# Up weight sums moved out of the output projection, down sums by whole blocks, residual loaded into the FFN accumulators, FFN memory laid out by first use

## The chip, the cores and the metric

The kernel runs on one core of a Trainium2 chip. The metric is device time in microseconds (us). The shown time before is the median of three runs. The profile is one further execution of the same program.

TensorE (PE) multiplies matrices into PSUM. VectorE (DVE), ScalarE (ACT) and GpSimd (POOL) do elementwise work. All DMAs here are issued from SyncE's queue (SP), in order: a DMA that waits for something holds up every DMA behind it.

## The reference, cut to what matters

One layer of an encoder for 2048 prompt tokens and 32 sample tokens, width 1024, FFN width 4096, all float32:

```python
z = rmsnorm(x, g_mix) @ w_in            # split into attention and GLA inputs
attn_o = sink_attend(...)               # windowed attention, head group A
gla_o, s_final = gla_chunked(...)       # gated linear attention, head group B
h = x + concat([attn_o, g]) @ w_out     # g: normed, gated gla_o
y = h + square(relu(rmsnorm(h, g_ffn) @ w_up)) @ w_down
```

## The kernel before, in words

Every large product is split in a high and a low float32r part (hi*hi, lo*hi, hi*lo). ACT writes the high part (a copy), POOL or DVE the low one (a subtraction).

**Stages.** Attention runs to about 340 us of the span, GLA to 727, the output projection (`op_phase`) to 900, the FFN (`ffn_phase`) to the end.

**The FFN** runs a Strassen-like scheme on 2x2 blocks: 7 products in place of 8. It takes three token groups in turn ("envs", 356, 356 and 328 columns), and for each of them 16 weight blocks of 256 rows of the FFN width. A block has 7 "up" steps U(b,0) to U(b,6), on the token tiles B11, B21, T2, T1, T3, B22, T4, and 7 "down" steps D(b,0) to D(b,6), on squared outputs uB11, uB22, uT1, uT3, uT2, uB21, uT4. A step has 12 products. U(0,0..6) come first; then D(g-1,i) and U(g,i) alternate. PE keeps this order; the order on the other engines is set by a scheduler that simulates the program. In env 0 all weights are loaded and split anew, with the weights of six steps prepared ahead (`AHEAD`).

**Sums of weights.** The scheme needs sums of weight quarters, S1 to S4. POOL makes them. Down sums (`block_sums`, L707, four operations a unit) are made in attention (5 blocks, in quarters of 128 columns), GLA (8 blocks, in halves) and the output projection (3 blocks, in halves), stored to `sd` in HBM and loaded again in the FFN. Up sums of blocks 1 to 8 (`up_sums`, L1161, four operations of 128x512 a block) are made in the output projection and stored to `su`. Those of blocks 0 and 9 to 15 are made in env 0 of the FFN itself (L1416); S2 and S3 are stored, S1 and S4 are made again in envs 1 and 2 by two operations.

**Output projection.** Six groups of columns, (p, gi) for three pieces and two halves. `post(p, gi)` normalizes a group; the second part of `post(p, 1)` writes the FFN's token tiles T1 to T4, B22 (and B11, B21 after gi = 0) to HBM (`Td`). That of the last group, `post(2,1)`, is left to the first steps of the FFN (`pending`) and uses the PSUM tiles `opa` and `opb`. The residual y goes to `yd`.

**FFN accumulators.** `P1` to `P7` (128x1424 each) take the down products. A first block copies into P2 to P5 (DVE, L1603), later ones add (DVE, L1509). `residual` (L1636, L1639) adds y from `yd` to P2 to P5 in blocks 2 to 9: 8 loads of 356 KB and 10 POOL additions an env. At an env's end `merge` (L1609, POOL) combines the accumulators and 16 stores write `out_yT`.

**Memory.** Pools are stacked: a tile laid on a pool that is gone waits for the last use of what lay there. Before, T1 and T2 lie over the mixer tiles, B11 and B21 over the first ones of these, T3, B22 and T4 over the projection's weights, and the first five slots of the ring of FFN weights (`wring`, pool `wfb`) over `opx`, where the stages of the up sums are. So the ring's first weights wait until the last `su` store has landed.

Of the kernel before, what the change touches and what calls it, by code (L numbers as in the profile page):

```python
# [62 lines left out]
class Builder:  # L63
# [641 lines left out]
    def block_sums(self, raw):  # L705

        tt = lambda o, x, y, op: self.G.tensor_tensor(out=o, in0=x, in1=y, op=op)  # L707
        a11, a21, a12, a22 = raw[:, 0, 0], raw[:, 0, 1], raw[:, 1, 0], raw[:, 1, 1]
        tt(a22, a21, a22, ALU.add)
        tt(a21, a11, a21, ALU.subtract)  # L710
        tt(a11, a22, a11, ALU.subtract)
        tt(a12, a12, a11, ALU.subtract)

    def down_sums(self, units, tile_, gap):

        w = self.a["w_down"].rearrange("(b k p) (m n) -> b p k m n", k=2, p=P, m=2)
        for b, c0, n in units:
            raw = tile_(f"sd{b}_{c0}")[:, : 4 * n].rearrange("p (k m n) -> p k m n", k=2, m=2)
            for k in range(2):
                self.Q.dma_start(raw[:, k], w[b, :, k, :, c0 : c0 + n])  # L720
            yield gap / 2
            self.block_sums(raw)
            yield gap / 2
# [423 lines left out]
    def up_raw(self, b, tile_=None):  # L1147

        w = self.a["w_up"].rearrange("(k p) n -> p k n", p=P)
        H = KB // 2  # L1150
        raw = []
        for k in range(2):
            x = (tile_ or self.io_tile)("stage").rearrange("p (k c) -> p k c", k=H)
            self.last_load = self.Q.dma_start(x, w[:, H * k : H * k + H, 256 * b : 256 * b + 256]).ins
            raw.append(x)
        return raw

    def up_sums(self, raw):

# [647 lines left out]
```

## Time and profile before

| | us |
|---|---|
| runs shown | 2284.13, 2289.86, 2290.94; median 2289.86 |
| profiled execution | 2278.04 |
| its span | 2276.1 |
| PE busy in the span | 2139.4 (94%) |
| DVE, ACT, POOL busy | 1577.8, 1230.9, 1436.6 |
| PE busy, 727 to 900 (output projection) | 168.18 of 173 |
| PE busy, 900 to 972 | 20.28 of 72 |

A row of the timeline gives start, length, engine, line, operation, output<-inputs and how many were merged; in brackets stands how long the engine was idle before it, and what ended that. The granted clock (PEclk) is a share of 2.4 GHz.

### The profile page before, as it was taken

The page shows a single profiled execution, that of the slowest core. Times are in us where ns is not written, and L with a number is a line of the kernel's source. Part 1 is how long each engine was busy: PE and PEld are TensorE (multiplying, and loading weights), DVE is VectorE, ACT ScalarE, POOL GpSimd, SP SyncE. Part 2 cuts the span into 40 slices and gives each one's busy share as a digit, 9 for nine tenths or more (in the row PEclk, how much of TensorE's full clock was granted, in tenths as well). Part 3 has the DMA queues.
Part 4 walks back from the last instruction along what each step waited for, and adds up shares of the span by engine and source line. Part 5 has one row for each costly group of instructions (what it writes and reads, how often), then busy time and mean ns, then how long its engine had stood idle before and what let it go on. Part 6 is the DMA issues. An engine that isn't in the chain of part 4 may idle for free.

```text
span 2276.1 us, 40775 instructions
## 1 busy us (share of the span) xinstructions
PE 2139.4 (94%) x14790; PEld 2007.6 (88%) x14790; DVE 1577.8 (69%) x3444; ACT 1230.9 (54%) x2728; POOL 1436.6 (63%) x1308
## 2 busy tenths in 40 slices
PE   7999999899989997399999998999999999999997
PEld 6777776788878997399999998999999999999996
DVE  8766666799896545457777777576666666676677
ACT  4555445556563222455666655666656666666662
POOL 5221356454462553646678779877787798788884
PEclk9999999899999999699999999999999999999999
DMA  7333576254435998654444448554444476555433
GB/s 267 138 119 107 197 229 196 94 172 140 152 120 176 326 339 317 235 189 153 155 150 136 130 134 302 178 158 152 150 142 131 139 288 194 163 161 155 157 108 117
DMA packets 245771, 402.03 MB, mean 177 GB/s; under 512 B 44721, under 2 KB 173026, under 8 KB 241730
## 3 DMA queue, kind: packets, MB, share of 16 engines
q1 hardware_dynamic: 245570, 399.44, 53.2%
q8 instruction: 116, 1.90, 0.3%
q14 instruction: 85, 0.70, 0.1%
HBM read 300.20 MB, written 99.18 MB: 175 GB/s over the span
## 4 chain that ended last, share of the span: by engine, by line
PE 54%; DVE 2%; DMA 2%; POOL 1%; ACT 0%; issue 0%; SPq 0%; ACTq 0%; POOLq 0%
PE dn L156 27%; PE u L156 27%; DVE P L1509 1%; DVE wf_d15A L1391 0%; DMA B22l<-Td2B 0%; DMA T3l<-Td0T 0%; DMA stage<-in_w_down 0%; DVE P L1609 0%; DMA Td2T<-y 0%; DMA ku0S<-wf_u0S 0%; DMA stage<-sd 0%; DVE u L1509 0%; POOL wf_u0S L1391 0%; DMA su<-stage 0%; POOL stage L1416 0%
## 5 line engine op out<-in xcount | busy, mean ns | idle before, releaser
L1509 DVE TENSOR_TENSOR P<-P,dn 128x712 f32<-128x712 f32 (+1 forms) x642 | 559.7, 875 | 234.7 <-PE dn L156 218.6
L43 ACT ACTIVATE u<-u 128x356 f32<-128x356 f32 (+1 forms) x384 | 174.1, 454 | 38.3 <-PE u L156 22.0
L707 POOL TENSOR_TENSOR sd<-sd 128x256 f32<-128x256 f32 (+1 forms) x168 | 110.7, 668 | 99.7 <-DMA sd<-in_w_down 93.4
L43 ACT ACTIVATE r<-u 128x356 f32<-128x356 f32 (+1 forms) x192 | 88.4, 461 | 136.3 <-PE u L156 136.2
L1509 DVE TENSOR_TENSOR u<-u,r 128x356 f32<-128x356 f32 (+1 forms) x144 | 75.7, 526 | 117.3 <-PE u L156 115.4
L938 POOL TENSOR_TENSOR E<-cc 128x256 f32<-128x256 f32 (+1 forms) x117 | 72.0, 648 | 67.3 <-DVE cc L790 43.5
L1014 DVE COPY_PREDICATED AT<-masks,A 64x64 f32<-64x64 int32 (+1 forms) x330 | 82.9, 253 | 14.2 <-ACT AT L43 4.7
L1609 POOL TENSOR_TENSOR P<-P,P 128x712 f32<-128x712 f32 (+1 forms) x38 | 64.9, 1728 | 26.3 <-DVE P L1509 26.1
L43 ACT ACTIVATE P<-S,negm 128x192 f32<-128x192 f32 (+2 forms) x128 | 51.5, 417 | 46.0 <-DVE negm L577 38.4
L595 POOL TENSOR_TENSOR P<-P,es 128x512 f32<-128x512 f32 x15 | 15.9, 1059 | 87.0 <-ACT sq L43 44.2
L1161 POOL TENSOR_TENSOR stage<-stage 128x512 f32<-128x512 f32 x32 | 42.9, 1344 | 43.0 <-DMA Td1T<-y 21.6
L43 ACT ACTIVATE E<-E 128x1024 f32<-128x1024 f32 (+2 forms) x68 | 67.3, 1012 | 2.8 <-POOL E L938 1.1
L949 DVE TENSOR_TENSOR E<-E,kq 128x256 f32<-128x256 f32 (+1 forms) x117 | 65.5, 615 | 1.1 <-ACT E L43 1.0
L1291 DVE TENSOR_TENSOR y<-op,y 128x356 f32<-128x356 f32 (+1 forms) x48 | 23.7, 517 | 58.0 <-PE op L156 37.8
L1416 POOL TENSOR_TENSOR stage<-stage 128x512 f32<-128x512 f32 x44 | 57.0, 1294 | 10.4 <-DMA stage<-in_w_up 5.0
L43 ACT ACTIVATE v<-go 128x256 f32<-128x256 f32 (+1 forms) x34 | 12.8, 380 | 75.7 <-DVE Sp L1046 43.3
L43 ACT ACTIVATE pS<-pT 128x256 f32<-128x256 f32 (+1 forms) x62 | 27.2, 489 | 46.9 <-PE pT L160 46.9
L576 DVE TENSOR_REDUCE mx<-S 128x2 f32<-128x384 f32 (+2 forms) x64 | 32.7, 536 | 26.8 <-PE S L156 26.5
L1509 DVE TENSOR_TENSOR u<-u,f 128x356 f32<-128x356 f32 (+1 forms) x96 | 49.8, 519 | 0.3 <-ACT u L43 0.2
L43 ACT ACTIVATE op<-y 128x356 f32<-128x356 f32 (+1 forms) x42 | 19.0, 466 | 50.3 <-DVE y L1291 50.3
L156 PE MATMUL u<-B11h,wf_u0A 128*128 128x356 f32 (+1 forms) x24 | 7.8, 392 | 38.3 <-ACT wf_u0A L43 37.9
L43 ACT ACTIVATE f<-u 128x356 f32<-128x356 f32 (+1 forms) x96 | 43.7, 455 | 0.0
(1899 smaller groups left out, 8820.9 us busy)
## 6 DMA issues: line engine op xcount, KB each, us to landing
stage<-in_w_up SPq DMA_DIRECT2D x108, 512.0 KB, 4.4
stage<-sd SPq DMA_DIRECT2D x92, 512.0 KB, 4.8
stage<-su SPq DMA_DIRECT2D x62, 512.0 KB, 4.0
...
```

The source lines that it names most:

```text
L43: ins = f(*args, **kw)
L156: self._pe(self.T.matmul(out, lhsT, rhs, start=start, stop=stop, **kw), ns)
L576: V.reduce_max(mx[:, ch, us], sp, axis=AX.X)
L707: tt = lambda o, x, y, op: self.G.tensor_tensor(out=o, in0=x, in1=y, op=op)
L938: G.tensor_tensor(out=e4, in0=c4, in1=ref, op=ALU.subtract)
L949: V.tensor_tensor(out=e4, in0=e4, in1=halves_of(kq, L, m), op=ALU.mult)
L1014: V.copy_predicated(dst, mk.unsqueeze(1).broadcast_to([L // nh, 2, w // m, m]), src[r].rearrange("s p (n m) -> s p n m", m=m),)
L1161: tt = lambda o, x, y, op: self.G.tensor_tensor(out=o, in0=x, in1=y, op=op)
L1291: V.tensor_tensor(out=y[:, f], in0=ps, in1=y[:, f], op=ALU.add)
L1416: tt = lambda o, x, y, op: G.tensor_tensor(out=o, in0=x, in1=y, op=op)
L1509: add = lambda out, x, y, op=ALU.add: V.tensor_tensor(out=out, in0=x, in1=y, op=op)
L1609: eng.tensor_tensor(out=e.acc[q][:, j : j + 2], in0=e.acc[q][:, j : j + 2], in1=e.acc[x][:, j : j + 2], op=ALU.add)
```

## The change

- Down sums: attention makes 4 blocks instead of 5, begun at step 3 instead of 9, with each POOL operation spawned by itself; GLA 6 instead of 8, in whole blocks (8 operations of 128x256 behind one pair of loads, one buffer); the output projection 6 instead of 3, in whole blocks (4 + 4 operations of 128x512 half a group apart).
- `up_raw` and `up_sums` are gone from the output projection with their 16 loads, 32 POOL operations and 16 stores. Blocks 1 to 8 are now made like 0 and 9 to 15, in the FFN: in env 0 four more POOL operations and one `su` store a block, in envs 1 and 2 two more POOL operations and one load less.
- `post` writes T2 and T4 into the group's own y0 tile, T3 into a buffer shared with z. The store of y[p][1]'s upper half is replaced by z = y_upper - y_lower, 12 new POOL operations of 128x356 in the projection.
- FFN pools are laid out by first use: T1 and T2 over the weights w_out half 0, T3 and B22 over half 1, T4 over the mixer tiles, the ring over `opx` (now two whole-block buffers).
- The residual is loaded into P2 to P5 by four DMAs of 712 KB (656 KB in env 2) an env at block 0, and block 0 of these four adds instead of copying. 8 loads and 10 POOL additions an env go.
- In block 15 of env 0 the low parts of A11 and A12 are made on POOL instead of DVE.

```diff
-EARLY, MIDDLE = 5, 8
+EARLY, MIDDLE = 4, 6
...
-            late = [(b, c0, 256) for b in range(EARLY, EARLY + MIDDLE) for c0 in (0, 256)]
-            two = lambda name: sums.tile([P, 1024], F32, tag="sd", name=name)
-            for j in range(2):
-                self.spawn(self.down_sums(late[j::2], two, 32000), 4000 + 16000 * j)
+            whole = lambda name: sums.tile([P, 2048], F32, tag="sd", name=name)
+            self.spawn(self.down_sums([(b, 0, 512) for b in range(EARLY, EARLY + MIDDLE)], whole, 2, 4500), 4000)
...
-                S.activation(t2[:, k], B, AF.Copy)
-                tt(t4[:, k], y0[:, H + k], B)
-            for x, src in (("T2", t2), ("T1", y[:, :H]), ("T3", t3), ("B22", y[:, H:]), ("T4", t4)):
+                S.activation(y0[:, k], B, AF.Copy)
+                tt(y0[:, H + k], y0[:, H + k], B)
+            for x, src in (("T2", y0[:, :H]), ("T4", y0[:, H:]), ("T1", y[:, :H]), ("T3", t3), ("B22", y[:, H:])):
...
-        todo += [("u", b, 0) for b in range(1, 9)]
...
+        for n, b in enumerate(range(EARLY + MIDDLE, self.NB)):
+            at = KB + 4 * n
+            steps.setdefault(at, []).append(lambda b=b: begin(b))
+            for i in (2, 3):
+                steps.setdefault(at + i, []).append(lambda b=b: more(b))
+            steps.setdefault(at + 6, []).append(lambda b=b: end(b))
...
+                        G.tensor_tensor(out=z[:, f - H], in0=y[:, f - H], in1=y[:, f], op=ALU.subtract)
...
+            tmem = tok(pool("toka"), ("T2", "T1"))
...
+            tmem |= tok(pool("tokb"), ("T3", "B22"))
+            wfa = pool("wfa")
...
+            tmem |= tok(pool("tokd"), ("B11", "B21"))
             wfc = pool("wfc")
-            wfb, sx = pool("wfb"), pool("sx")
+            amem |= {i: mem(pool(f"acc{i}"), H * NM, f"P{i}", F32) for i in (3, 5, 7, 6, 2, 4)}
+            umem["T4"] = upair(pool("ud"), "T4")
+            wfb, xa, sx = pool("wfb"), pool("xa", bufs=2), pool("sx")
...
-                    eng = V if n == 0 and i in (0, 5) else G
+                    eng = V if n == 0 and i in (0, 5) and not keep else G
...
-                        if b:
+                        if b or q not in (1, 6, 7):
                             add(at, at, ps)
...
+                if b or i not in (0, 1, 4, 5):
                     return
...
+                q = DOWN[i + 1][2]
+                gi, f0 = {2: (0, 0), 3: (1, 0), 4: (0, H), 5: (1, H)}[q]
+                Q.dma_start(envs[n].acc[q], self.yd[envs[n].p][gi][:, f0 : f0 + H])
```

Three places show how the order moves, all on SP.

First the end of the output projection. `su` are the stored up sums, `ku0` are stores of split weights of block 0 for the later envs, `stage` are loads of raw weights. SP before:

```order
L59 DMA T3l_10874<-Td1T3_201 128x1424 [waits DMAHW7_49]
L59 DMA B22l_10876<-Td1B22_202 128x1424 [waits DMAHW0_49]
L59 DMA stage_10362<-in_w_up 128x4x256 [waits DMAHW1_49]
L59 DMA T4l_10878<-Td1T4_203 128x1424 [waits DMAHW2_49]
L59 DMA ku0A22_11051<-wf_u0A22_11048 128x1024 [waits DMAHW3_49,Pool_49]
L59 DMA stage_10472<-in_w_up 128x4x256 [waits DMAHW4_49]
L59 DMA stage_10474<-in_w_up 128x4x256 [waits DMAHW5_49]
L59 DMA su70_166<-stage_10360 128x1024 [waits DMAHW6_49,Pool_49]
L59 DMA su71_167<-stage_10362 128x1024 [waits DMAHW7_49,DMAHW1_49,Pool_49]
L59 DMA su80_168<-stage_10472 128x1024 [waits DMAHW4_49,DMAHW0_49,Pool_49]
L59 DMA su81_169<-stage_10474 128x1024 [waits DMAHW5_49,Pool_49]
L59 DMA ku0A11_10950<-wf_u0A11_10947 128x1024 [waits DMAHW2_49,DMAHW6_49,DMAHW1_49,DMAHW7_49,DMAHW0_49,Pool_49]
```
SP after, same place:

```order
L59 DMA T2l_10721<-Td1T2_199 128x1424 [waits DMAHW6_49,PE_49]
L59 DMA T1l_10723<-Td1T1_200 128x1424 [waits DMAHW7_49]
L59 DMA Td2B21_205<-y20_9863 128x1424 [waits DMAHW0_49,DVE_49]
L59 DMA T3l_10741<-Td1T3_201 128x1424 [waits DMAHW1_49,PE_49]
L59 DMA B22l_10743<-Td1B22_202 128x1424 [waits DMAHW2_49]
L59 DMA yd21_189<-y21_10289 128x1424 [waits DMAHW4_49,DMAHW3_49,DVE_49]
L59 DMA T4l_10756<-Td1T4_203 128x1424
L59 DMA yd21_189<-z2_10607 128x1424 [waits DMAHW5_49,Pool_49]
L59 DMA ku0S4_10857<-wf_u0S4_10854 128x1024 [waits DMAHW6_49,Pool_49]
L59 DMA ku0A22_10928<-wf_u0A22_10925 128x1024 [waits DMAHW7_49,Pool_49]
L59 DMA stage_11605<-in_w_up 128x4x256 [waits DMAHW0_49]
L59 DMA su10_154<-stage_11010 128x1024 [waits DMAHW1_49,Pool_49]
```
The eight `su` stores and the loads for them are gone from between T4l and the first weights' stores; T2l and T1l, and then T3l, now wait for PE, yd21 and z2 stand around T4l.

Second the end of `post(2,1)`, some 60 to 70 us later in the span before. Td2 are the stores of its results, P the accumulators. SP before:

```order
L59 DMA Td2B22_209<-y21_10437 128x1424 [waits DMAHW4_49,DVE_49]
L59 DMA Td2T3_208<-tT3_9244 128x1424 [waits DMAHW5_49,DVE_49]
L59 DMA Td2T1_207<-y21_10437 128x1424 [waits DMAHW6_49,Activation_49]
L59 DMA Td2T2_206<-tT2_9243 128x1424 [waits DMAHW7_49,Activation_49]
L59 DMA Td2T4_210<-tT4_9245 128x1424 [waits DMAHW0_49,DVE_49]
L59 DMA stage_11287<-in_w_down 128x1024 [waits DMAHW1_49,DVE_49]
L59 DMA stage_11401<-in_w_down 128x512 [waits DMAHW3_49,DMAHW2_49,Pool_49]
```
SP after:

```order
L59 DMA Td2B22_209<-y21_10289 128x1424 [waits DMAHW3_49,DVE_49]
L59 DMA Td2T3_208<-T32_10698 128x1424 [waits DMAHW4_49,DVE_49]
L59 DMA Td2T1_207<-y21_10289 128x1424 [waits DMAHW5_49,Activation_49]
L59 DMA Td2T2_206<-y20_9863 128x1424 [waits DMAHW6_49,Activation_49]
L59 DMA Td2T4_210<-y20_9863 128x1424 [waits DMAHW7_49,DVE_49]
L59 DMA P4_10805<-yd10_186 128x1424 [waits DMAHW4_49,DMAHW0_49,PE_49]
L59 DMA P2_10801<-yd10_186 128x1424 [waits DMAHW5_49,DMAHW3_49,DMAHW1_49]
L59 DMA stage_11283<-in_w_down 128x512 [waits DMAHW2_49,Pool_49]
L59 DMA P3_10785<-yd11_187 128x1424 [waits DMAHW7_49,DMAHW6_49]
L59 DMA P5_10789<-yd11_187 128x1424
```
The four loads P<-yd now follow the Td2 stores, the last two of them wait for the queue slots of the last stores, and stage loads follow.

Third the change from env 0 to env 1, where the results of env 0 are stored. SP before:

```order
L59 DMA out_yT_prompt<-P3_10931 128x356 [waits DMAHW5_49,Pool_49]
L59 DMA out_yT_prompt<-P3_10931 128x356 [waits DMAHW6_49]
L59 DMA out_yT_prompt<-P2_10930 128x356 [waits DMAHW7_49,DVE_49]
L59 DMA out_yT_prompt<-P2_10930 128x356 [waits DMAHW0_49]
L59 DMA out_yT_prompt<-P3_10931 128x356 [waits DMAHW1_49,Pool_49]
L59 DMA out_yT_prompt<-P3_10931 128x356 [waits DMAHW2_49]
L59 DMA stage_16083<-in_w_down 128x1024 [waits DMAHW3_49,Pool_49]
L59 DMA out_yT_prompt<-P5_10933 128x356 [waits DMAHW4_49,Pool_49]
L59 DMA out_yT_prompt<-P5_10933 128x356 [waits DMAHW5_49]
```
SP after:

```order
L59 DMA out_yT_prompt<-P3_10785 128x356 [waits DMAHW5_49,Pool_49]
L59 DMA out_yT_prompt<-P3_10785 128x356 [waits DMAHW6_49]
L59 DMA out_yT_prompt<-P2_10801 128x356 [waits DMAHW7_49,DVE_49]
L59 DMA out_yT_prompt<-P2_10801 128x356 [waits DMAHW0_49]
L59 DMA out_yT_prompt<-P3_10785 128x356 [waits DMAHW1_49,Pool_49]
L59 DMA out_yT_prompt<-P3_10785 128x356 [waits DMAHW2_49]
L59 DMA P2_10801<-yd20_188 128x1424 [waits DMAHW4_49,DMAHW7_49,DMAHW3_49,DMAHW0_49]
L59 DMA P3_10785<-yd21_189 128x1424 [waits DMAHW5_49,DMAHW6_49,DMAHW2_49,DMAHW1_49]
L59 DMA stage_15872<-sd0_136 128x1024 [waits Pool_49]
L59 DMA out_yT_prompt<-P5_10789 128x356 [waits Pool_49]
```
The loads of P2 and P3 stand between the stores and wait for them; stage loads, and the stores of P5 and P4, are behind.

## Rows read from the trace of the kernel before

**Rows 1.** Stages of the span: busy time of each engine (with instruction counts), granted PE clock, share of the DMA engines' time, GB/s.
```profile
0.00:340.00 340.00, 322.81 (x1804) 252.49 (x1805) 233.08 (x843) 167.41 (x511) 122.25 (x204) 0.98 0.52 176
340.00:727.00 387.00, 354.86 (x3839) 300.13 (x3838) 318.73 (x963) 213.80 (x417) 196.39 (x259) 0.96 0.45 146
727.00:900.00 173.00, 168.18 (x1071) 167.44 (x1069) 88.84 (x222) 42.97 (x84) 79.92 (x66) 0.99 0.94 317
900.00:972.00 72.00, 20.28 (x101) 19.02 (x100) 24.60 (x51) 25.44 (x49) 41.58 (x31) 0.62 0.70 272
1385.00:1445.00 60.00, 49.34 (x286) 48.07 (x286) 40.47 (x49) 33.99 (x68) 55.33 (x39) 0.94 0.75 265
```

**Rows 2.** Timeline of PE from the projection's last product to the step D(0,2).
```profile
899.78 0.32 PE L156 MATMUL op<-mx1h,wo11l 128*128 128x356 f32 x1
...
938.04 0.67 PE L156 MATMUL u<-B11h,wf_u0A 128*128 128x356 f32 x1 [37.94 <-ACT wf_u0A L43]
...
942.53 1.26 PE L156 MATMUL oprb<-ones,acc 128*89 128x1 f32 x8
...
972.42 0.67 PE L156 MATMUL dn<-uB11h,wf_d0A 128*128 128x356 f32 x1 [13.81 <-ACT wf_d0A L43]
...
979.30 0.33 PE L156 MATMUL dn<-uB22h,wf_d0S 128*128 128x356 f32 x1
...
983.19 0.32 PE L156 MATMUL dn<-uT1h,wf_d0S 128*128 128x356 f32 x1
```

**Rows 3.** Timeline of ACT, POOL and SP in the first of these gaps.
```profile
921.55 1.48 ACT L43 ACTIVATE T4h<-T4l 128x712 fp32r<-128x712 f32 x2 [1.59 <-DMA T4l<-Td1T]
937.37 1.15 ACT L43 ACTIVATE wf_u0A<-stage 128x512 fp32r<-128x512 f32 x2 [14.34 <-DMA su<-stage]
927.01 7.59 POOL L1161 TENSOR_TENSOR stage<-stage 128x512 f32<-128x512 f32 x6
928.29 6.66 SPq L59 DMA_DIRECT2D su<-stage  x4
```

**Rows 4.** Timeline of DVE (first and last operation of the second part of `post(2,1)`), SP (its last two stores) and ACT (the first operation behind them).
```profile
950.84 0.59 DVE L1225 SCALAR_TENSOR_TENSOR opa<-y,packed,oprb 128x356 f32<-128x356 f32 x1 [0.37 <-PE oprb L156]
967.89 0.53 DVE L1237 TENSOR_TENSOR tT<-y,opb 128x356 f32<-128x356 f32 x1 [0.53 <-ACT tT L43]
967.89 1.73 SPq L59 DMA_DIRECT2D Td2T<-tT  x2
975.47 0.47 ACT L43 ACTIVATE uT3h<-u 128x356 fp32r<-128x356 f32 x1 [3.10 <-DMA Td2T<-tT]
```

**Rows 5.** DMA issues: KB each and median us from issue to landing, the first row from 896 to 984 us, the others from 1360 to 1450 us.
```profile
T4l<-Td1T SPq DMA_DIRECT2D x1, 712.0 KB, 13.6
...
out_yT_prompt<-P SPq DMA_DIRECT2D x16, 178.0 KB, 3.1
...
B11l<-Td2B SPq DMA_DIRECT2D x1, 712.0 KB, 4.0
...
T4l<-Td2T SPq DMA_DIRECT2D x1, 712.0 KB, 8.6
```

**Rows 6.** Timeline of PE and DVE at the first product of the projection's last group that waited.
```profile
888.12 0.43 PE L156 MATMUL op<-mx1h,wo10h 128*128 128x356 f32 x1 [1.54 <-DVE y L1291]
887.53 2.27 DVE L1291 TENSOR_TENSOR y<-op,y 128x356 f32<-128x356 f32 x5 [6.70 <-DMA y<-in_xT_prompt]
```

**Rows 7.** GLA: who waited for whom (us in total, times, longest), and groups by line (count, busy us, mean ns).
```profile
PE dk L160 <- DVE AT L961: 9.5, 3, 5.8
POOL sd L707 <- DMA sd<-in_w_down: 71.2, 11, 21.1
L707 POOL TENSOR_TENSOR sd<-sd 128x256 f32<-128x256 f32 (+1 forms) x89 | 63.1, 715 | 74.7 <-DMA sd<-in_w_down 71.2
L949 DVE TENSOR_TENSOR E<-E,kq 128x256 f32<-128x256 f32 (+1 forms) x117 | 65.5, 615 | 1.1 <-ACT E L43 1.0
```

**Rows 8.** Timeline of PE, DVE and SP at the change from env 0 to env 1, and of PE at that from env 1 to env 2 (last row).
```profile
1392.62 0.60 PE L156 MATMUL dn<-uB22h,wf_d15S 128*128 128x356 f32 x2 [2.55 <-POOL wf_d15S L1391]
1401.17 9.38 DVE L1391 TENSOR_TENSOR wf_d15A<-stage,wf_d15A 128x512 fp32r<-128x512 f32 x1
1411.41 0.67 PE L156 MATMUL dn<-uT2h,wf_d15S 128*128 128x356 f32 x1 [7.13 <-DVE P L1509]
1402.96 3.38 POOL L1507 TENSOR_TENSOR T4l<-T4l,T4h 128x712 fp32r<-128x712 f32 x2
1426.83 8.40 SPq L59 DMA_DIRECT2D out_yT_prompt<-P  x8
1841.40 0.40 PE L156 MATMUL dn<-uB22h,wf_d15S 128*128 128x356 f32 x1 [1.26 <-ACT B22h L43]
```

**Rows 9.** Durations by line (ns shortest/median/longest, first and last start), and one stretch of env 0 with blocks whose up sums are made there (columns as in rows 1).
```profile
L1416 POOL TENSOR_TENSOR stage<-stage x44: 1273/1294/1313, 841.6 to 2214.4; 128x512 f32<-128x512 f32 x44
L1636 POOL TENSOR_TENSOR P<-P,stage x24: 1591/1725/2126, 1036.5 to 2118.9; 128x712 f32<-128x712 f32 x16, 128x656 f32<-128x656 f32 x8
L1603 DVE COPY P<-dn x24: 841/899/901, 980.5 to 1890.2; 128x712 f32<-128x712 f32 x16, 128x656 f32<-128x656 f32 x8
L1509 DVE TENSOR_TENSOR P<-P,dn x642: 824/895/899, 1003.9 to 2266.5; 128x712 f32<-128x712 f32 x107, 128x656 f32<-128x656 f32 x54
1275.00:1300.00 25.00, 25.00 (x156) 25.00 (x155) 18.42 (x28) 14.66 (x32) 18.42 (x15) 1.00 0.40 133
```

More of the change, by code (lines that the diff above doesn't have):

```diff
@@ L703, in load_gla_consts, with block_sums, load_block, down_sums @@
         self.gla_consts = masks, d0, wal, bal, one, ones
[L705 to L714, printed above, removed]
+    def block_sums(self, raw, parts=1):
+        n = raw.shape[-1] // parts
+        for i in range(parts):
+            part = raw[:, :, :, i * n : (i + 1) * n]
+            a11, a21, a12, a22 = part[:, 0, 0], part[:, 0, 1], part[:, 1, 0], part[:, 1, 1]
+            for o, x, y, op in ((a22, a21, a22, ALU.add), (a21, a11, a21, ALU.subtract), (a11, a22, a11, ALU.subtract), (a12, a12, a11, ALU.subtract)):
+                self.G.tensor_tensor(out=o, in0=x, in1=y, op=op)
+                yield
+    def load_block(self, raw, b, c0, n):
         w = self.a["w_down"].rearrange("(b k p) (m n) -> b p k m n", k=2, p=P, m=2)
+        for k in range(2):
+            self.Q.dma_start(raw[:, k], w[b, :, k, :, c0 : c0 + n])
+    def down_sums(self, units, tile_, parts, step):
         for b, c0, n in units:
             raw = tile_(f"sd{b}_{c0}")[:, : 4 * n].rearrange("p (k m n) -> p k m n", k=2, m=2)
[L719 to L723, printed above, removed]
+            self.load_block(raw, b, c0, n)
+            yield 6000
+            for _ in self.block_sums(raw, parts):
+                yield step
+            yield 6000
             with self.tc.issue_after(self.Q.last.ins):
@@ L1145, in size @@
         return sum(t1 - t0 for _, t0, t1 in g)
[L1147 to L1158, printed above, removed]
-        A = lambda m, k: raw[k - 1][:, :, (m - 1) * P : m * P]
-        tt = lambda o, x, y, op: self.G.tensor_tensor(out=o, in0=x, in1=y, op=op)
-        tt(A(2, 2), A(2, 1), A(2, 2), ALU.add)
-        tt(A(2, 1), A(1, 1), A(2, 1), ALU.subtract)
-        tt(A(1, 1), A(2, 2), A(1, 1), ALU.subtract)
-        tt(A(1, 2), A(1, 2), A(1, 1), ALU.subtract)
     def keep_sums(self, b, raw):
@@ L1176, in op_phase @@
         nt, H = self.nt, KB // 2
[L1177 to L1178 removed]
+        m1 = pool("opm1", 1)
         mem1 = [m1.tile([P, KB * REST + 272], F32R, tag=x, name=f"mx1{x}") for x in "hl"]
@@ L1294, in op_phase @@
                     V.tensor_tensor(out=acc, in0=acc, in1=ps, op=ALU.add)
-                if f % H == H - 1:
-                    hs = slice(f - H + 1, f + 1)
-                    Q.dma_start(self.yd[p][gi][:, hs], y[:, hs])
+                if gi and f >= H:
+                    if f == H:
+                        z = stage(f"z{p}", N)
+                    G.tensor_tensor(out=z[:, f - H], in0=y[:, f - H], in1=y[:, f], op=ALU.subtract)
+                if f == H - 1 and not gi:
+                    Q.dma_start(self.yd[p][gi][:, :H], y[:, :H])
+                if f == KB - 1:
+                    if gi:
+                        Q.dma_start(self.yd[p][gi][:, :H], z)
+                    Q.dma_start(self.yd[p][gi][:, H:], y[:, H:])
                 if f in (1, 2) and pending is not None:
@@ L1303, in op_phase @@
                     next_mix(*groups[j + 1])
-                if j and f in (1, 3, 5, 7):
-                    sums()
-            pending = post(p, gi, acc)
-        while raws:
-            sums()
+                for step in steps.pop(KB * j + f, ()):
+                    step()
+            pending = post(p, gi, acc, stage(f"T3{p}", N) if gi else None)
         self.pending = pending
@@ L1653, in ffn_phase @@
                 else:
+                    residual(g, i)
                     down(g, i)
```

91 lines of the change are left out of this document (28 added, 63 removed).

## The prediction

> **What bounds the kernel now.** First the stages [rows 1]: PE is the bound nearly everywhere and stands still in few places. In attention and GLA it misses 340.00 − 322.81 = 17.2 and 387.00 − 354.86 = 32.1 us; in the projection 4.8. Between 900 and 972 us it works 20.28 us of 72, at a granted clock of 0.62 (near the lower level, 1.2 GHz), and at the change of env 49.34 of 60. So one hole of some 60 us, one of 10, and many small ones are all there is to win.
>
> Then the timeline of PE in the hole [rows 2]. I call the end of the projection E = 900.1 (899.78 + 0.32). U(0,0) starts at 938.04 after 37.94 us, D(0,0) at 972.42 after 13.81 us more, and the regular alternation is reached with D(0,2) at 983.19 = E + 83.1. PE had slow products after each gap: D(0,0) and U(1,0) take 972.42 to 979.30 = 6.9 us, where the next two, D(0,1) and U(1,1), take 979.30 to 983.19 = 3.9. The yardstick: a product is 1.95 us, the seven of U(0) are 13.6.
>
> Who ended the first gap? Of four candidates in [rows 3] the tokens are not it: T4h is ready at 923.0 and POOL goes on. ACT's split of the first weights waits till 937.37 for "su<-stage", the last stores of the up sums. These are held by POOL's six operations, 7.59 us to 934.6, and the weight ring lies on the memory that they leave. The chain is loads, sums, stores, memory, weights, PE. Who ended the second? The second part of `post(2,1)`, 17.5 us of DVE and ACT (950.84 to 968.42), then two stores issued to 969.62, then ACT, which resumes at 975.47, 5.85 us after the last issue [rows 4].
>
> **The change part by part.**
>
> *Up sums out of the projection.* 32 POOL operations at 7.59 / 6 = 1.27 us are 41 us, with 16 loads and 16 stores of 512 KB, in a stage whose DMA share is 0.94 [rows 1, 3]. The ring no longer waits for them. By the order its first weights are split and stored ahead of E; B11 and B21 wait for group (2,0) alone, T2 and T1 for half a group. So U(0,0) starts at E, not E + 37.9.
>
> *What is late next.* (1) T3 and B22 lie over the second half of w_out and are loaded from E. A 712 KB load lands in 4.0 to 8.6 us, 13.6 in the crowd of the hole [rows 5]. U(0,4) needs T3 at E + 7.8, so I expect a stall of 2 to 4 us for transfer and split, some 5 with T4; nothing hides it, and U(0) ends near E + 18. (2) `post(2,1)`: its square sums stand behind U(0,0), at 942.53, and from there to the first `opa`, 950.84, it took 8.3 us [rows 2, 4]; but DVE's split of T4 now stands ahead of `opa`. T4 is issued at about E + 2; with 8.6 us to land and 1.5 for T4h [rows 3] `opa` starts at E + 12.5 (E + 17 with 13.6; with 4.0 the square sums are last, at about E + 10). 17.5 us later, E + 30, the PSUM tiles are free: D(0,0) at E + 31. (3) Then come D(0,0), U(1,0) at the slow clock again, 6.9, and D(0,1), U(1,1), 3.9: D(0,2) at E + 42. (4) The residual loads come behind the last Td2 store: issue by E + 32, landing 5.85 later as in [rows 4], then 4.0 or a little more for P3 [rows 5]: E + 42 to E + 43, just when D(0,1) wants to add into it. Two independent reasons give the same time, which I take: **E + 42, 41 us gained**. Bounds: with T4 and P3 at 4.0, E + 10 + 17.5 + 2 + 5.85 + 4.0 = E + 39; with T4 at 13.6 and P3 at 8.6, E + 17 + 17.5 + 2 + 5.85 + 8.6 + 1 = E + 52, gain 31. If neither blocks PE, U(0) and the four products (7.8) end between E + 21.4 without any token stall and E + 26 with it, say E + 24, and the gain is 59.
>
> *Up sums inside the FFN.* Eight blocks get four POOL operations of 1.29 us in env 0 (41 us) and two in envs 1 and 2 [rows 9]. The cover is POOL's idle time: blocks that do this already have POOL at 18.42 of 25 us with PE at 25.00 [rows 9]. The ten residual additions of 1.73 us leave at the same time. I cost this at 0, at most 4. Without that cover it would be 41.
>
> *First copy to addition on DVE.* 899 against 895 ns [rows 9]: 0.
>
> *Last group of the projection.* y21 was late by 6.70 us on DVE, 1.54 of which reached PE [rows 6], while the DMA share was 0.94. With the up sums' 32 transfers of 512 KB gone (16.8 MB) and three more down blocks added, 1 MB in and 1 MB out each (6 MB) I take −1.5 (0 to −1.5). The twelve operations for z are POOL's in time that the up sums leave free: 0.
>
> *Down sums in attention and GLA.* Attention has 64 quarter operations instead of 80, GLA 48 half operations instead of 64. 16 × 0.715 = 11.4 us of POOL leave GLA [rows 7], where DVE is busy 318.73 of 387 and so near the bound [rows 1]. L949 takes 615 ns on average while POOL shares the stage [rows 7], which I hold to be lengthened by it. Against it stands the head of the line: POOL waited 71.2 us for loads of sums, once 21.1, and everything POOL does for GLA stands behind. I take −5, from −15 (half of GLA's holes) to +5.
>
> *Changes of env.* First env 0 to 1. PE waited 2.55 for a split of d15, and 7.13 behind DVE, whose split of d15A12 took 9.38 us while POOL worked without a pause (T4l, 1402.96, and the rows around it) [rows 8]. Moved to POOL, that gap should mostly go: −5 of the 7.13, since POOL's queue grows by two splits and one sum, 3 × 1.29 = 3.9, ahead of d15S3 and d15S2. The Trainium skill ("SBUF — State Buffer", "Who interferes with whom") says that a DVE operation with two SBUF inputs and a GpSimd one that reads SBUF exclude each other for a whole instruction. The row agrees in kind and not in size: one POOL operation would be 1.7 us and the split 2.4, yet 9.38 were measured, so the lock was not handed over between POOL's instructions. Had the rule the size right, the move would be worth under 2 instead of 5 here and the sum would be 3 worse.
>
> The residual loads add a cost. SP issues the eight stores in 8.40 us [rows 8], each lands in 3.1 and the load in 4.0 to 8.6 [rows 5], and the load waits for the stores from the same tile; before, the accumulator was free when its store had landed. So P3 is ready 4 to 8.6 later, of which PE's short PSUM buffer hides a part: +5.5, at both changes. Together −5 + 5.5 + 5.5 = **+6**, from 0 (the additions wait, PE doesn't) to +15 (both loads at 8.6, lock not relieved). The second change had gaps of only some 1.26 [rows 8], so all of it would show there as new.
>
> **Sum.** −41 − 1.5 − 5 + 6 + 0 = −41.5 against the profiled execution: 2278.0 − 41.5 = 2236.5. The median of the runs is 11.8 above that execution, so 2248.4, say **2248**.
>
> **The rivals.**
>
> *The hole closes nearly whole.* Post's results and P3 arrive in time, and D(0,2) is at E + 24: −59 − 1.5 − 5 + 6 = −59.5, 2230. For it: everything of U(0) is prepared. Against: 17.5 us of `post` and its stores are not shortened by any part of the change. 0.12.
>
> *The residual loads cost more.* They land at 13.6 as T4l did in the crowd: D(0,2) at E + 55, gain 28, and each change of env +7.5: −28 − 1.5 − 5 + 15 = −19.5, 2270. For it: four loads of 712 KB in a row, at a moment at which Td stores and weight loads run. Against: the hole's crowd was made of the sums' transfers, which leave. 0.12.
>
> *The sums only move.* POOL becomes the bound of env 0 and gives back 41: no change, 2289. Against it stands POOL at 18.42 of 25 [rows 9]. 0.04, to which I add 0.03 for a mix of the last rival and this one, ending within the noise.
>
> *Slower: POOL's head of the line in GLA.* A whole block is a pair of 512 KB loads into one buffer that must be stored first, and then eight operations, 8 × 0.7 = 5.7 us. If POOL stands before a load as it did (21.1 at worst [rows 7]) with E behind it, DVE and then PE starve, as in the 9.5 us that dk waited for DVE [rows 7]. At 10 us a block the six blocks cost 60: −41 − 1.5 + 60 + 6 = +23.5, 2313. It decides from 36.5 / 6 = 6 us a block. Against: each operation is now spawned 4.5 us apart, 6 us after its loads, and before, with more units, all of GLA's holes were 32.1 us. 0.06.
>
> **How the numbers follow.** The forecast has 0.63, the closed hole 0.12, dear loads 0.12, unchanged 0.07, slower 0.06. The independent bounds around 2248 (hole −10 or +10, GLA ±10, envs −6 or +9) together, as a root of squares, give some 17 either way; with the two neighbours on the faster side, the range is 2228 to 2272. A difference of 0.3%, 6.9 us, is about what a measurement of this kernel can tell from no change. Faster 0.87, same 0.07, slower 0.06.
>
> **What would show it.** In the profile after: U(0,0) directly behind the last product of the projection, a gap of 2 to 5 us at T3 or T4, one of about 13 before D(0,0), D(0,2) at E + 39 to E + 52; no wait for "su<-stage"; POOL near 20 of 25 us in blocks 1 to 8 of env 0 with PE at 25.00; the operation of 9.38 us gone; a wait of DVE for "P<-yd" at the changes of env. I am wrong if PE waits for POOL inside env 0, if D(0,1) waits for P3 long after `post`, or if GLA's span grows.

## The result and the profile after

| | us |
|---|---|
| runs of the changed kernel | 2273.32 to 2278.25, median 2273.91 (5 runs) |
| runs of the kernel before | 2284.13 to 2294.04, median 2289.86 (5 runs) |
| ratio, 95% interval | 0.9941, 0.992 to 0.9962 |
| profiled execution, before and after | 2278.04 and 2273.91 |

The change makes the kernel 0.6% faster, 16 us by the medians, 4.1 by the two profiled executions. I had forecast 2248 with a range to 2272.

The stages of the changed kernel (windows: time, busy PE, PEld, DVE, ACT, POOL with counts, granted clock, DMA share, GB/s):

```profile
340.00:700.00 360.00, 337.57 (x3742) 285.71 (x3740) 299.78 (x947) 207.77 (x406) 156.40 (x205) 0.96 0.36 122
700.00:775.00 75.00, 51.30 (x314) 50.00 (x315) 25.25 (x58) 13.11 (x27) 31.67 (x29) 0.84 0.90 297
775.00:912.50 137.50, 133.97 (x825) 133.35 (x824) 71.03 (x175) 37.42 (x70) 66.39 (x47) 0.97 0.78 270
912.50:959.30 46.80, 28.86 (x149) 28.04 (x149) 26.89 (x60) 27.19 (x56) 26.78 (x20) 0.78 0.76 282
959.30:1369.00 409.70, 408.27 (x2496) 407.98 (x2496) 297.93 (x439) 251.44 (x527) 310.69 (x240) 1.00 0.41 137
1369.00:1418.50 49.50, 38.09 (x217) 36.66 (x217) 25.53 (x39) 23.56 (x50) 49.50 (x36) 0.92 0.86 304
```

The hole of [rows 1, 2] from 900 to 983 us has become one of 46.8 us, with 18 lost in it. But the projection, which missed 4.8 of 173 us, now misses 27 of 212, 23.7 of them in its first 75.

The timeline of PE, at the products that waited (the first and the sixth row bound the projection; U(0,0) is at 914.69, D(0,0) at 945.30, D(0,2) at 959.26):

```profile
700.24 0.42 PE L156 MATMUL op<-m0h,wo10l 128*128 128x328 f32 x1 [1.38 <-POOL wo10l L270]
...
738.76 1.25 PE L156 MATMUL oprb<-ones,acc 128*82 128x1 f32 x8 [15.05 <-issue]
...
767.83 0.43 PE L156 MATMUL op<-mx0h,wo00h 128*128 128x356 f32 x1 [2.95 <-ACT mx0h L43]
...
772.82 0.67 PE L156 MATMUL op<-mx0l,wo00h 128*128 128x356 f32 x1 [4.56 <-POOL mx0l L1113]
...
833.18 0.43 PE L156 MATMUL op<-mx1h,wo10h 128*128 128x356 f32 x1 [3.52 <-DVE y L1271]
...
912.17 0.33 PE L156 MATMUL op<-mx1h,wo11l 128*128 128x356 f32 x1
...
914.69 0.40 PE L156 MATMUL u<-B11h,wf_u0A 128*128 128x356 f32 x1 [2.20 <-issue]
...
945.30 0.64 PE L156 MATMUL dn<-uB11h,wf_d0A 128*128 128x356 f32 x1 [11.79 <-DVE y L1218]
...
959.26 0.40 PE L156 MATMUL dn<-uT1h,wf_d0S 128*128 128x356 f32 x1 [3.95 <-DVE P L1496]
...
1418.48 0.64 PE L156 MATMUL dn<-uT3h,wf_d0S 128*128 128x356 f32 x1 [6.95 <-DVE P L1496]
...
1859.92 0.42 PE L156 MATMUL dn<-uT1h,wf_d0S 128*128 128x328 f32 x1 [2.31 <-DVE P L1496]
...
1871.58 0.64 PE L156 MATMUL dn<-uT3h,wf_d0S 128*128 128x328 f32 x1 [6.25 <-DVE P L1496]
```

Before, the product that bounds the projection, and the one with the gap of 15.05, stood at

```profile
715.28 0.42 PE L156 MATMUL op<-m0h,wo10l 128*128 128x328 f32 x1 [1.41 <-POOL wo10l L270]
...
742.06 0.72 PE L156 MATMUL oprb<-ones,acc 128*82 128x1 f32 x8 [3.29 <-issue]
```

PE's order is the same in both kernels from there on, so the starts of the same products give the account. S is the product above, E the end of the projection's last product. The stages are: S; S to E; E to D(0,2); on to D(15,1) of env 0; on to D(0,3) of env 1; on to D(0,3) of env 2; on to the end. All in us, from the trace of each run:

| run | S | S to E | to D(0,2) | to D(15,1) | change 1 | env 1, change 2 | rest |
|---|---|---|---|---|---|---|---|
| before | 715.3 | 184.8 | 83.1 | 406.4 | 47.3 | 439.3 | 399.9 |
| after | 700.2 | 212.3 | 46.8 | 409.9 | 49.4 | 453.1 | 400.6 |
| forecast, difference | −5 | −1.5 | −41 | 0 | +0.5 | +5.5 | 0 |
| measured, difference | −15.0 | +27.4 | −36.3 | +3.5 | +2.0 | +13.8 | +0.7 |
| a_resid | 700.4 | 212.6 | 42.9 | 408.0 | 42.6 | 442.0 | 401.6 |
| a_gate | 699.8 | 196.2 | 48.8 | 410.9 | 49.6 | 453.2 | 400.8 |
| a_y00 | 697.4 | 209.0 | 47.3 | 409.5 | 49.9 | 452.1 | 402.0 |
| a_best | 697.4 | 197.1 | 46.7 | 408.4 | 42.1 | 440.8 | 401.6 |
| a_best2 | 702.1 | 197.2 | 46.0 | 408.3 | 42.3 | 441.9 | 401.6 |
| a_tok | 690.5 | 195.0 | 42.7 | 408.2 | 42.3 | 442.5 | 401.5 |
| b_noup | 716.9 | 183.1 | 49.5 | 406.0 | 49.7 | 439.6 | 402.5 |
| b_noup46 | 706.1 | 178.0 | 50.3 | 406.0 | 50.1 | 439.6 | 403.1 |
| b_46d | 709.0 | 178.0 | 52.9 | 407.5 | 43.0 | 444.2 | 404.4 |
| b_46t | 704.5 | 178.0 | 44.5 | 407.7 | 42.8 | 443.3 | 403.8 |
| b_mix | 700.4 | 182.6 | 48.1 | 407.7 | 42.5 | 443.9 | 403.9 |
| b_d15 | 719.6 | 184.8 | 83.5 | 407.6 | 41.9 | 440.1 | 399.7 |

The main step came out close, 36 of 41 us. The projection gave 27 of them back. From S to E the two kernels have the same 1138 matmuls on PE (windows of before, then of after; columns as in [rows 1]):

```profile
715.28:900.10 184.82, 179.07 (x1138) 177.68 (x1138) 92.52 (x230) 44.46 (x87) 85.25 (x71) 0.99 0.93 312
```

```profile
700.24:912.49 212.25, 185.26 (x1138) 183.34 (x1138) 96.28 (x233) 50.53 (x97) 97.83 (x74) 0.93 0.82 280
```

So 21.2 of the 27.4 us are longer waits (27.0 instead of 5.8), and 6.2 are slower products, at a granted clock of 0.93 instead of 0.99.

### The profile page after: what moved, and what is told of

The parts are those of the page before. It is cut to its first block, busy times and chain, and to the rows that moved or that the text cites. A ratio compares the mean times of both kernels' runs of the same rounds, so it can differ in the third digit from the quotient of the medians.

```text
span 2272.1 us, 40454 instructions
## 1 busy us (share of the span) xinstructions
PE 2150.4 (95%) x14790; PEld 2018.8 (89%) x14790; DVE 1560.5 (69%) x3442; ACT 1231.3 (54%) x2728; POOL 1433.5 (63%) x1292
## 4 chain that ended last, share of the span: by engine, by line
PE 53%; POOL 2%; DVE 2%; DMA 1%; issue 1%; ACT 0%; SPq 0%; POOLq 0%; DVEq 0%; ACTq 0%
PE dn L156 27%; PE u L156 26%; DVE P L1496 1%; POOL P L1594 1%; DMA out_yT_prompt<-P 0%; POOL wf_d0S L1378 0%; DMA T3l<-Td0T 0%; DMA T1l<-Td2T 0%; DVE P L1594 0%; POOL wf_u1S L1378 0%; DVE u L1496 0%; DMA P<-yd 0%; POOL B22l L1494 0%; POOL wf_d15S L1378 0%; POOL T3l L1494 0%
## 5 line engine op out<-in xcount | busy, mean ns | idle before, releaser
L1496 DVE TENSOR_TENSOR P<-P,dn 128x712 f32<-128x712 f32 (+1 forms) x666 | 580.9, 875 | 261.5 <-PE dn L156 227.3
L712 POOL TENSOR_TENSOR sd<-sd 128x128 f32<-128x128 f32 (+2 forms) x136 | 107.0, 806 | 88.4 <-DMA sd<-in_w_down 83.8
L1403 POOL TENSOR_TENSOR stage<-stage 128x512 f32<-128x512 f32 x92 | 119.3, 1297 | 23.8 <-DMA stage<-in_w_up 17.3
L43 ACT ACTIVATE v<-go 128x256 f32<-128x256 f32 (+1 forms) x34 | 12.8, 380 | 75.7 <-DVE Sp L1052 44.5
L955 DVE TENSOR_TENSOR E<-E,kq 128x256 f32<-128x256 f32 (+1 forms) x117 | 51.4, 491 | 1.4 <-ACT E L43 1.4
L844 POOL TENSOR_TENSOR g<-g,ggla 128x512 f32<-128x512 f32 (+1 forms) x17 | 22.6, 1344 | 40.3 <-ACT g L43 40.3
L156 PEld LDWEIGHTS A<-E 64*64 64x64 f32 (+1 forms) x1704 | 32.5, 147 | 6.7 <-issue 4.7
```

Source lines behind the costliest of these rows:

```text
L43: ins = f(*args, **kw)
L156: self._pe(self.T.matmul(out, lhsT, rhs, start=start, stop=stop, **kw), ns)
L844: G.tensor_tensor(out=gv, in0=gv, in1=ggla[:r].unsqueeze(1).broadcast_to([r, 4, P]), op=ALU.mult)
L955: V.tensor_tensor(out=e4, in0=e4, in1=halves_of(kq, L, m), op=ALU.mult)
L1403: tt = lambda o, x, y, op: G.tensor_tensor(out=o, in0=x, in1=y, op=op)
L1496: add = lambda out, x, y, op=ALU.add: V.tensor_tensor(out=out, in0=x, in1=y, op=op)
```

## The experiments

Runs named a_ start from the changed kernel, b_ from the kernel before. Ratios are against the kernel before on the same chip.

**a_resid: the residual as before.**

```diff
...
-                Q.dma_start(envs[n].acc[q], self.yd[envs[n].p][gi][:, f0 : f0 + H])
...
+                if i == 0:
+                    waiting[g] = load(self.yd[e.p][gi][:, f : f + 2])
+                if DOWN[i][2] == q:
+                    y, j = waiting.pop(g), f % H
+                    at = e.acc[q][:, j : j + 2]
+                    G.tensor_tensor(out=at, in0=at, in1=y, op=ALU.add)
...
```

Block 0 copies into P2 to P5 again, too.

> The changed kernel with one part undone: the residual comes again by 8 small loads and POOL additions an env in blocks 2 to 9 (8 additions, since the stored difference z is used), and block 0 copies into P2 to P5. Theory (the residual loads into the accumulators cost what the changes of env lost): the waits of PE behind 'DVE P' at D(0,2) (3.95 us), at D(0,3) of env 1 (6.95) and at D(0,2) and D(0,3) of env 2 (2.31 and 6.25) go, and the slow products behind them; profiled execution 2252 to 2258 us instead of 2273.9, ratio to the kernel before 0.984 to 0.988. Rival (the accumulators are late anyway, since stores of the results and POOL's longer queue hold them): the gaps stay within 3 us of these sizes, ratio 0.992 to 0.996.

Measured: 2251.17 median, ratio 0.9839 (0.9819 to 0.986), just beyond the 0.984 to 0.988 that I expected. By the traces the span is 22.0 us shorter than after, and 22.5 us shorter from E on. In the changed kernel, at the first change of env, SP issued and DVE waited thus (timeline):

```profile
1412.11 0.33 SPq L59 DMA_DIRECT2D P<-yd  x1
...
1417.44 1.70 DVE L1496 TENSOR_TENSOR P<-P,dn 128x712 f32<-128x712 f32 x2 [5.01 <-POOL wf_d0A L1378]
```

POOL is named there, but the operation needs nothing of it. The load landed at that time, at 1417.32; the four of this stretch took

```profile
P<-yd SPq DMA_DIRECT2D x4, 712.0 KB, 5.3
```

In a_resid the same step copies, and waits only for the store that leaves the accumulator (timeline):

```profile
1407.38 0.90 DVE L1590 COPY P<-dn 128x712 f32<-128x712 f32 x1 [0.73 <-DMA out_yT_prompt<-P]
...
1850.47 0.41 PE L156 MATMUL dn<-uT3h,wf_d0S 128*128 128x328 f32 x1 [0.87 <-ACT P L43]
```

The wait of 6.25 us at the second change is 0.87. The theory holds: the loads cost 3.8 us in the hole, 1.8 in env 0, 6.8 and 11.1 at the changes of env, and took 1.0 off the rest.

**a_gate: the first group's y ahead of the others, down sums held back; a_y00: the first of these alone.**

```diff
+                if (p, gi) == (0, 0):
+                    self.y00 = Q.dma_start(yt[:, :, off : off + t1 - t0], src).ins
+                else:
+                    with tc.issue_after(self.y00):
+                        Q.dma_start(yt[:, :, off : off + t1 - t0], src)
...
-            at = KB + 4 * n
+            at = KB + 2 + 4 * n
...
-            self.load_block(x, b, 0, 512)
+            with tc.issue_after(Q.last.ins):
+                self.load_block(x, b, 0, 512)
```

> The changed kernel with another order of loads in the output projection: the loads of y for the first group go ahead of those for the next two groups, and each whole-block load of down sums is traced two products later and queued behind the last DMA traced ahead of it. Theory (the projection lost 27 us because y of its first group, then the mixer tiles of the third group, come behind loads that are not yet needed, and POOL's sums stand ahead of the splits): the gap of 15.05 us falls to 6 or less, those of 2.95, 4.56 and 3.52 mostly go, the projection ends at 893 to 900 us instead of 912.5, profiled execution 2255 to 2262. Rival (the memory of the first y is free only when GLA's last stores have landed, so no order helps): the gap of 15.05 stays above 10 and the projection ends after 906.

> The changed kernel with the first group's y ahead of the next groups' y alone; the whole-block loads of down sums are not held back, and four of them now come ahead of the first y. Theory (the order of y is most of the 15.05 us): the gap falls to 4 to 8 us. Rival (the crowd of whole-block loads is most of it): it stays above 10.

In the changed kernel the gap of 15.05 us hangs on y of the first group. Ten prompt loads of y are issued from 706.62 on. By their sizes the first seven belong to the next two groups, and the first group's own three and its sample load stand behind them; the whole-block loads of down sums come after that (timeline of SP and DVE):

```profile
706.62 1.31 SPq L59 DMA_DIRECT2D y<-in_xT_prompt  x2
...
709.33 14.51 SPq L59 DMA_DIRECT2D y<-in_xT_prompt  x8
723.88 1.54 SPq L59 DMA_DIRECT2D y<-in_xT_sample  x1
725.46 3.15 SPq L59 DMA_DIRECT2D sd<-in_w_down  x4
...
728.96 3.37 DVE L1271 TENSOR_TENSOR y<-op,y 128x328 f32<-128x328 f32 x8 [4.71 <-DMA y<-in_xT_sample]
```

The product that waits for it, in a_y00 and then in a_gate (timeline of PE):

```profile
731.94 1.25 PE L156 MATMUL oprb<-ones,acc 128*82 128x1 f32 x8 [11.06 <-issue]
```

```profile
726.77 1.25 PE L156 MATMUL oprb<-ones,acc 128*82 128x1 f32 x8 [3.47 <-issue]
```

a_gate: 2268.42 median, ratio 0.991 (0.9883 to 0.9936), the profiled execution at 2261.05; E at 896.0 instead of 912.5. a_y00: one run, 2268.77, E at 906.4. By its number a_y00 speaks for its rival, since the gap stayed above 10. But the run doesn't decide between the two: in it four whole-block loads, which stand behind y in the changed kernel, moved ahead of it. With these held back too, in a_gate, 3.47 are left, 7.6 less than in a_y00. The kernel before has 3.29 at this product. So of the 15.05 some 11.8 were new, and a_gate takes back 11.6. No run has the order of the y's alone; that the seven loads ahead are what y waits for in the changed kernel is read from the rows above. The gap of 3.52 went too; those at the third group, 2.94 and 4.33, did not, where I expected that they mostly would. That the new places in memory put y of the first group last is not shown: no run moves the layout alone. None of the b_ runs, which keep the old layout and the projection's sums by halves, has a gap over 3.4 there.

**a_best: a_resid and a_gate together; a_best2: besides, the third group's mixer tiles ahead of its y.**

```diff
-                if f == (0 if gi else 2) and j + 1 < len(groups):
-                    load_y(*groups[j + 1])
-                if f == 1 and 2 <= j + 1 < len(groups):
+                if f == (0 if j == 1 else 1) and 2 <= j + 1 < len(groups):
                     next_mix(*groups[j + 1])
+                    if j == 1:
+                        self.y00 = Q.last.ins
+                if f == (0 if gi else 2) and j + 1 < len(groups):
+                    load_y(*groups[j + 1])
```

> The changed kernel with both earlier edits: the residual by small loads and POOL additions, and the first group's y ahead of the other loads with the down sums' loads held back. Theory (the two losses are independent, 22 us at the accumulators and 13 to 16 in the projection): profiled execution 2234 to 2240 us, ratio 0.976 to 0.982, the projection ends at 893 to 898 us, no wait of PE for the residual. Rival (they share a cause, the queue's order, and one repairs part of the other): 2245 or more.

> As a_best, with the loads of the third group's mixer tiles also queued ahead of that group's y. Theory (the two gaps of 2.94 and 4.33 us at the start of the third group are late mixer tiles behind four loads of y): both fall below 1 and the projection ends 5 to 7 us earlier than in a_best. Rival (the tiles are late because ACT's copies and POOL's subtractions of them stand behind POOL's down sums): the gaps stay, the projection ends within 2 us of a_best.

a_best: 2235.06 median, ratio 0.9772 (0.9734 to 0.981): the two losses add up. a_best2: ratio 0.9776 (0.9743 to 0.9809), the projection as long (197.2 against 197.1), both gaps unchanged, so that theory fell; its rival forecast the time, but not the owner. In a_best ACT copies the tiles when PE has ended the group before (timeline):

```profile
751.83 2.86 ACT L43 ACTIVATE mx0h<-m 128x128 fp32r<-128x128 f32 x4 [2.62 <-PE op L156]
```

With the old layout, in b_noup46, its four copies begin from 10 to 19 us earlier, though S is 8.7 us later there, and wait for loads only; the second of them:

```profile
735.26 1.06 ACT L43 ACTIVATE mx0h<-m 128x1024 fp32r<-128x1024 f32 x1 [1.84 <-DMA m<-mixT]
```

The pool `opm0` now begins where `opm1` lay, and the wait for PE points to a tile that the second group still reads there. No run moved that pool alone, so this owner is read from the trace, not shown by a run.

**b_noup: the up sums out of the projection, alone.**

```diff
-        todo += [("u", b, 0) for b in range(1, 9)]
```

> The kernel before with one part alone: the up sums of blocks 1 to 8 are not made in the output projection, so that they are made in env 0 of the FFN. Theory (the first gap of 37.94 us hung on the su stores alone, and POOL has room in env 0): that gap falls to 8 to 15 us (now the token tiles), D(0,2) comes 55 to 65 us after the last product of the projection instead of 83, env 0 stays at full PE busy, ratio 0.987 to 0.992. Rival (POOL becomes the bound of env 0): blocks 1 to 8 of env 0 take 3 us longer each, ratio above 0.996.

2257.76 median, ratio 0.9862 (0.9832 to 0.9892). One line gives more than the whole change. PE at U(0,0), U(0,6) and D(0,0) (timeline):

```profile
902.21 0.40 PE L156 MATMUL u<-B11h,wf_u0A 128*128 128x356 f32 x1 [2.26 <-issue]
...
925.57 0.43 PE L156 MATMUL u<-T4l,wf_u0A 128*128 128x356 f32 x1 [2.57 <-POOL T4l L1506]
...
939.76 0.66 PE L156 MATMUL dn<-uB11h,wf_d0A 128*128 128x356 f32 x1 [13.12 <-ACT wf_d0A L43]
```

The gap of 37.94 is 2.26, better than the 8 to 15 I expected. The token tiles are still late, but inside U(0) and by less: PE waits 0.84, 1.36 and 2.57 us for POOL's splits of T3, B22 and T4. D(0,2) comes at E + 49.5, where I expected 55 to 65. Env 0 takes 406.0 us as before (406.4), so the added POOL operations cost nothing.

**b_noup46: besides, 4 and 6 blocks of down sums ahead of the projection.**

```diff
-EARLY, MIDDLE = 5, 8
+EARLY, MIDDLE = 4, 6
```

> The kernel before without the up sums in the projection, and with 4 blocks of down sums in attention and 6 in GLA, so 6 in the projection, all still in the small units of before. Theory (GLA became 15 us shorter in the changed kernel because POOL has 16 operations less there, which DVE no longer shares SBUF with): the first projection product that waits comes 10 to 15 us earlier than the 715.5 us of the run with 5 and 8 blocks. Rival (it is the spreading: whole blocks and single operations spawned apart): it comes less than 4 us earlier.

2242.99 median, ratio 0.9806 (0.9774 to 0.9839). S at 706.1, and 709.0 and 704.5 in the two runs below with the same counts; with the old counts it was 715.3, 716.9 and 719.6. The means, 706.5 and 717.3, differ by 10.7 us: the counts. The changed kernel and the six a_ runs, which have one code up to there and also spread the operations, have 690.5 to 702.1, on average 698.3.

**b_d15: the low parts of d15A11 and d15A12 on POOL, alone.**

```diff
-                    eng = V if n == 0 and i in (0, 5) else G
+                    eng = V if n == 0 and i in (0, 5) and not keep else G
```

> The kernel before with one part alone: in block 15 of env 0 the low parts of d15A11 and d15A12 are made on POOL instead of DVE. Theory (DVE could not get in between POOL's back-to-back operations, 9.38 us for an operation of 0.69): the PE gap of 7.13 us at D(15,4) goes, POOL's queue makes the gap at D(15,1) (2.55) up to 3 us longer, D(0,3) of env 1 comes 4 to 8 us earlier. Rival (each engine waits for one instruction of the other at most, so under 2 us of the 9.38 came from sharing, and the rest of the gap has another owner): D(0,3) of env 1 comes less than 2 us earlier. Both give a ratio between 0.996 and 1.0; the trace tells them apart.

Ratio 0.9999 (0.9976 to 1.0023), so the runs' times show nothing; the trace decides. PE and DVE there (timeline):

```profile
1398.18 0.60 PE L156 MATMUL dn<-uB22h,wf_d15S 128*128 128x356 f32 x2 [2.16 <-POOL wf_d15S L1391]
...
1404.60 3.31 DVE L1509 TENSOR_TENSOR P<-P,dn 128x712 f32<-128x712 f32 x4 [0.44 <-PE dn L156]
```

The operation of 9.38 us [rows 8] and the PE gap of 7.13 are gone, change 1 takes 41.9 us instead of 47.3, and env 0 1.2 more: −4.2, and −5.6 between b_noup46 and b_46d. The theory holds.

**b_46d: b_noup46 with b_d15. b_46t and a_tok: T3, B22 and T4 of the first env split on POOL only, in b_46d and a_best. b_mix: b_46t with the change's spreading of down sums in attention and GLA.**

```diff
-                load_tok(envs[0], t, (V, G))
+                load_tok(envs[0], t, (G, G) if t in ("T3", "B22", "T4") else (V, G))
```

> The kernel before with three parts of the change alone: no up sums in the projection, 4 and 6 blocks of down sums ahead of it, and d15A11 and d15A12 on POOL. Theory (these parts carry the change's gain, and the memory by first use, the whole blocks and the residual loads add nothing to it): profiled execution 2228 to 2234 us, ratio 0.976 to 0.981, as fast as the best mended form of the changed kernel (0.9772) or faster. Rival (the layout by first use is worth several us on its own): ratio 0.982 or more.

> As b_46d, with the low parts of T3, B22 and T4 of the first env all on POOL, so that DVE's queue has no token split ahead of or between the operations of post(2,1). Theory (the gap before D(0,0) is post's 17.5 us, and it starts late because DVE waits for tokens): D(0,0) comes 2 to 4 us earlier against the last product of the projection than in b_46d, where I expect 39 to 40 us. Rival (POOL is then late with T3 and T4, and PE waits there instead): D(0,0) within 1 us.

> As a_best, with the low parts of T3, B22 and T4 of the first env all on POOL. Theory: the first operation on opa comes 2 to 4 us earlier after the projection's last product than the 17.8 us of a_best, and D(0,0) (36.8 us there) as much. Rival: POOL's longer queue stalls U(0,4) and U(0,6) and D(0,0) stays within 1 us.

> As b_46t, with the spreading of the change in attention and GLA: begun at step 3, whole blocks in GLA, each POOL operation spawned apart. Theory (the count of blocks brought about 11 us to GLA and the spreading about 8 more): the first projection product that waits comes at 695 to 700 us instead of the 704.5 to 709.0 of the three runs with the same counts in small units, and the projection takes 178 us as there, ratio 0.971 to 0.975, the fastest so far. Rival (whole blocks at the end of GLA are still under way when the projection begins and crowd its first loads): the projection takes 185 us or more and eats the gain, ratio as in b_46t.

b_46d: 2236.52, ratio 0.977 (0.9747 to 0.9794), in the range expected, though its profiled execution, 2240.76, was above the 2228 to 2234 I gave. b_46t: 2236.12, 0.9774 (0.9756 to 0.9793), D(0,0) at E + 35.0 instead of 42.2, and the first operation on `opa` at E + 15.0 instead of 17.9. The gap ahead of D(0,0), in b_46d and b_46t (PE):

```profile
929.21 0.67 PE L156 MATMUL dn<-uB11h,wf_d0A 128*128 128x356 f32 x1 [11.30 <-ACT wf_d0A L43]
```

```profile
917.57 0.67 PE L156 MATMUL dn<-uB11h,wf_d0A 128*128 128x356 f32 x1 [5.27 <-ACT wf_d0A L43]
```

a_tok: 2229.04, ratio 0.9748 (0.9715 to 0.9782), `opa` at E + 12.9 instead of 17.8 and D(0,0) at E + 33.0 instead of 36.8. So the traces bear out that token splits on DVE delay `post`. The size is less sure: with the splits unchanged D(0,0) came at E + 34.6 in a_gate, 35.8 in a_best2, and 39.7 in b_noup46. The runs' times don't tell b_46t from b_46d. b_mix: 2232.53, 0.9758 (0.973 to 0.9787); S at 700.4, just past the 695 to 700 of its theory; the projection is 4.6 us longer, where the rival says 7 or more; and the ratio lies between the two. So neither is settled. These four, a_best and a_best2 lie between 0.9748 and 0.9776 and can't be told apart; all beat the changed kernel and the kernel before.

## Why the prediction was wrong, point by point

- **"U(0,0) starts at E."** Right: E + 2.2, and no wait for "su<-stage" is left in the hole. b_noup shows the mechanism alone.
- **"What is late next."** Right in its chain, and in part by luck: `opa` at E + 14.2 (12.5 expected), D(0,0) at E + 32.8 (31), then D(0,1) waits for P3. The stall of 2 to 5 us at T3 or T4, one of the signs that I had named, did not come: U(0) waited for no token. It ended at E + 21.0 all the same (18 expected), since it began 2.2 late and ran its first 5.3 us at a granted clock of 0.58, near the lower level of 1.2 GHz. D(0,2) came at E + 46.8 instead of 42. P3 has the third of the four residual loads, which is issued at E + 39.8 (timeline of SP; I had E + 32), so that P3 was later than D(0,1) by 3.95 us:

```profile
946.36 2.44 SPq L59 DMA_DIRECT2D P<-yd  x2
951.91 0.33 SPq L59 DMA_DIRECT2D stage<-in_w_down  x1
952.34 0.86 SPq L59 DMA_DIRECT2D P<-yd  x2
```

- **"Up sums inside the FFN: 0."** Right: 406.0 against 406.4 us in b_noup, and in the changed kernel PE is busy 408.27 of 409.70 us with POOL at 310.69.
- **"Last group of the projection: −1.5."** This is the step that failed. The wait that I priced did go, but no other part of the projection had a term: the new order of its loads and its new memory stood at nothing, without a reason. It lost 27.4 us: 11.8 more than before at the first group, where, by the trace, y now comes behind seven loads that are needed later; 7.5 where the third group's tiles meet memory that is still read, also by the trace alone; 3.5 at y of the fourth; less the 1.5 at the last; and 6.2 in slower products behind these gaps. The order of SP in the trace shows the first of these, and I had argued from the projection's end alone. a_gate gives 16 of the 27 back.
- **"Changes of env: +6."** The mechanism was right on both counts; the price of the loads was too low, which is the second step that failed. d15 on POOL gave −4.2 to −5.6 (−5). The loads cost 22.5 us in all by a_resid, where I had 5.5 twice: at the second change two of them wait one after the other (2.31 and 6.25), and slow products follow, with a granted clock of 0.66 in the 5.1 us behind the first wait and 0.65 in the 4.4 us behind the second.
- **"Down sums in attention and GLA: −5."** Right in sign, too small: −15.0, the end of my range. The counts bring 10.7 by the means of three runs each. The rest comes with the spreading: b_mix, which adds it to the old layout, has S at 700.4 against 706.5. L949 had a mean of 615 ns [rows 7]; after, the same operation reads (page, costliest groups)

```profile
L955 DVE TENSOR_TENSOR E<-E,kq 128x256 f32<-128x256 f32 (+1 forms) x117 | 51.4, 491 | 1.4 <-ACT E L43 1.4
```

  which fits POOL's smaller part in GLA. With the smaller counts alone it is between, in b_noup46 (page, costliest groups; b_noup, with the old counts, has 584):

```profile
L949 DVE TENSOR_TENSOR E<-E,kq 128x256 f32<-128x256 f32 (+1 forms) x117 | 56.5, 537 | 1.6 <-ACT E L43 1.6
```

- **The sum.** −41.5 forecast; the misses are −10 (GLA), +28.9 (projection), +4.7 (hole), +3.5 (env 0: 1.8 from the loads, 1.2 from d15 by b_d15), +1.5 and +8.3 (changes), +0.7: −3.9, as the two spans show (2276.1 and 2272.1). The measured 2273.91 lies 1.9 us past my range, but the account was further off than that: −10 in GLA covers a third of the miss in the projection. Of the rivals, "the residual loads cost more" was true at the changes of env (+15.8 in all, against its +15) and gave 2270. That its sum is near is luck: its hole of E + 55 did not come, and no rival had the projection's loss.
- **From the profile to the median.** I added 11.8 us because the profiled execution of before was that much below its median. After, it is the median (both 2273.91). Executions of one code differ already at S: 715.3, 716.9 and 719.6 with the code of before, 690.5 and 697.4 for a_tok and a_best, which do not differ up to there. The profile is one draw, and such a difference is not a term to carry over.
